# Differential-attention units: output, squares and emission one step later in the attention pipeline

## The chip, the cores and the metric

The kernel runs on one core of a Trainium2 chip. The metric is the device time of one execution in microseconds (us). A core has a matrix engine (TensorE, PE in the profile; PEld is its weight load), a vector engine (VectorE, DVE), a scalar engine (ScalarE, ACT), GpSimd (POOL) and a queue that issues transfers (SyncE, SP). Each engine takes its instructions strictly in order. Matmuls and transposes write to PSUM, of which the kernel uses eight banks of 128 x 512 floats; the other engines read the results from there.

## The reference

Two layers of a decoder trunk on a sequence of 1024 rows of width 1024. Each layer projects the normalised stream to the columns of three groups of heads, runs them, gates them, and maps them back. Only group A is touched by the change:

```python
s1 = jnp.einsum('bhqd,bhkd->bhqk', q1b, k1).astype(jnp.float32) * scale
s2 = jnp.einsum('bhqd,bhkd->bhqk', q2b, k2).astype(jnp.float32) * scale
p1 = jax.nn.softmax(jnp.where(causal, s1, -jnp.inf), axis=-1)
p2 = jax.nn.softmax(jnp.where(causal, s2, -jnp.inf), axis=-1)
w = (p1 - lam * p2).astype(v.dtype)
oa = jnp.einsum('bhqk,bhkd->bhqd', w, v)
...
oa = oaf * lax.rsqrt(jnp.mean(jnp.square(oaf), -1, keepdims=True) + SUBLN_EPS) * subln_g * (1.0 - lam_init)
ya = _from_blocks(oa) * jax.nn.silu(ag)
```

Group B is softmax attention with a forget bias, group C stick-breaking attention. Then `h = LayerNorm(alpha * h + y @ w_out)`.

## The kernel before

**Units and blocks.** In each layer attention is cut into eight units that follow each other: C0, C1 (a pair of heads each), A0, A1, A2, A3 (one differential head each), B0, B1 (a pair each). A unit has eight blocks of 128 query rows. Block i of group A has i+1 key tiles, so blocks grow from 0 to 7; B runs from 7 down to 0.

**Stages of a block (`attn_a`).** `soft` makes two sets of scores on TensorE (tiles S), a maximum and a shift on VectorE (`neg_max`, L300), the exponential on ScalarE (L331), and combines both softmaxes into one weight tile e_A (L334 to L336, VectorE). `turn` transposes that tile on TensorE (tiles T, L310) and copies it back over e_A: the first 512 columns on ScalarE (L312), the rest on VectorE (L314). `mix` multiplies it with the values on TensorE (tile O_A) and copies the result to ou_A (L352, VectorE). `close`, once for four blocks, has ScalarE square the four results (sq_A, L363), GpSimd raise to the power -1/2 (rsa_A, L367) and VectorE scale them (L369). `emit` transposes the four (To_A, L378) and writes y_A (L379, VectorE).

**The steps.** `advance` makes one step: it starts one new block and runs the later stages of blocks that were started before. How many steps behind its start a block's stage runs is the table LAG (soft, turn, mix, close, emit); the order of the stages in one step is ORDER, which is emit, close, mix, soft, turn:

```python
LAG = {"A": (0, 2, 3, 4, 6), "B": (0, 1, 2, 3, 5), "C": (0, 1, 2, 3, 5)}
DEEPEST, LAST = 6, 4
ORDER = {"A": (4, 3, 2, 0, 1), "B": (4, 3, 2, 0, 1), "C": (4, 3, 2, 0, 1)}
```

**Steps between projections.** Beside a unit the kernel computes the projections that later units need (FOLLOW): beside A1 these are q and k of A2 and the gate of A0, beside B0 q of B1, the gate of A3 and k of B1. A step is put between matmuls of the projection (tiles acc_...; acr_... for values) whenever the attention's share of its estimated time falls behind the projection's share. A gate needs its unit finished: before it, steps are made until the unit's last block has been emitted, with no projection between them. The q and k of group A go through the rotary tables on VectorE (L275 to L278) and are then split into two parts, one on ScalarE (L204), one on VectorE (L206 for k, L208 for q).

**Buffers and order.** A scheduler lays the written program out on each engine and hands out buffers; it may take a later matmul before an earlier one that it holds not to be ready. What matters here: "T" has two PSUM banks, and T, O_A, To_A and O_B all live in them; "S" has four banks; "e" has six buffers in SBUF (a block of A takes two in `soft` and keeps one until `mix`; a block of B takes two and keeps both until `mix`).

Of the kernel before, what the change touches and what calls it, by code (L numbers as in the profile page):

```python
# [39 lines left out]
SCORE_US = [2 * sum(0.0945 if b - a == P else (b - a) / 2370 for a, b in row_pieces((i + 1) * P)) for i in range(NB)]  # L40

PACE = 8.0
LAG = {"A": (0, 2, 3, 4, 6), "B": (0, 1, 2, 3, 5), "C": (0, 1, 2, 3, 5)}
DEEPEST, LAST = 6, 4
ORDER = {"A": (4, 3, 2, 0, 1), "B": (4, 3, 2, 0, 1), "C": (4, 3, 2, 0, 1)}
PARTNER = list(range(8, 16)) + list(range(8)) + list(range(16, 32))

# [2 lines left out]
def tile_trunk(ctx, tc, x, ln_in_g, ln_in_b, w_in, b_forget, lambda_q1, lambda_k1, lambda_q2,  # L50
# [581 lines left out]
    for layer in range(DEPTH):  # L632
# [66 lines left out]
        def advance():  # L699
            nonlocal cursor  # L700
            cost = 0.0
            for stage in ORDER[pipe[min(cursor, len(pipe) - 1)][0][0]]:
                for at in range(max(0, cursor - DEEPEST), min(cursor + 1, len(pipe))):
                    u, blk = pipe[at]
                    if cursor - at != LAG[u[0]][stage]:
                        continue
# [97 lines left out]
```

## Time and profile before

| what | us |
|---|---|
| median of 3 executions | 1359.32 (1358.81 to 1362.91) |
| the profiled execution | 1358.92 |
| its span, first to last instruction | 1357.1 |
| TensorE busy in the span | 1323.9 |
| VectorE busy | 858.4 |
| ScalarE busy | 581.1 |
| GpSimd busy | 304.8 |

The profiled execution lies 0.40 below the median, and 1.8 of it lie outside the span. Busy times of engines overlap. The end of a matmul in the profile is modelled, so start times of following matmuls tell more than durations. Times in the rows below are counted from the start of the span.

### The profile page before, as it was taken

The page shows a single profiled execution, that of the slowest core. Times are in us where ns is not written, and L with a number is a line of the kernel's source. Part 1 is how long each engine was busy: PE and PEld are TensorE (multiplying, and loading weights), DVE is VectorE, ACT ScalarE, POOL GpSimd, SP SyncE. Part 2 cuts the span into 40 slices and gives each one's busy share as a digit, 9 for nine tenths or more (in the row PEclk, how much of TensorE's full clock was granted, in tenths as well). Part 3 has the DMA queues.
Part 4 walks back from the last instruction along what each step waited for, and adds up shares of the span by engine and source line. Part 5 has one row for each costly group of instructions (what it writes and reads, how often), then busy time and mean ns, then how long its engine had stood idle before and what let it go on. Part 6 is the DMA issues. An engine that isn't in the chain of part 4 may idle for free.

```text
span 1357.1 us, 21998 instructions
## 1 busy us (share of the span) xinstructions
PE 1323.9 (98%) x8258; PEld 1132.8 (83%) x8258; DVE 858.4 (63%) x1913; ACT 581.1 (43%) x1329; POOL 304.8 (22%) x313
## 2 busy tenths in 40 slices
PE   8999999999999999999999999999999999999997
PEld 6988888987898888877798898898789888888886
DVE  6635577569765775856532538574887657768554
ACT  3345454435444544541214444544444545556100
POOL 4220211111122131233412111012111212221432
PEclk9999999999999999999999999999999999999999
DMA  7551212121213232243515111112121222232332
GB/s 268 167 162 42 63 40 67 48 66 40 63 28 103 55 94 64 101 125 129 171 70 156 47 48 40 55 48 78 40 56 47 65 81 63 63 117 101 119 134 82
DMA packets 116342, 115.41 MB, mean 85 GB/s; under 512 B 8646, under 2 KB 94602, under 8 KB 116236
## 3 DMA queue, kind: packets, MB, share of 16 engines
q1 hardware_dynamic: 116236, 114.01, 28.3%
q8 instruction: 65, 1.06, 0.3%
q14 instruction: 41, 0.34, 0.1%
HBM read 74.63 MB, written 22.05 MB: 71 GB/s over the span
## 4 chain that ended last, share of the span: by engine, by line
PE 45%; DVE 5%; ACT 2%; DMA 2%; issue 1%; POOL 0%; DVEq 0%; ACTq 0%; POOLq 0%; SPq 0%
PE aco_o L72 11%; PE acr_vvA L72 3%; PE acc_ggA L72 3%; PE acc_qA L72 3%; PE O_A L72 2%; PE S_A L72 2%; PE acc_kA L72 2%; PE acr_vvC L72 2%; PE acc_ggB L72 2%; PE acc_kB L72 2%; PE acr_vvB L72 2%; PE acc_ggC L72 1%; PE acc_qB L72 1%; PE acc_kC L72 1%; PE O_C L72 1%
## 5 line engine op out<-in xcount | busy, mean ns | idle before, releaser
L72 PE MATMUL aco_o<-wo,yhi_o 128*128 128x512 f32 (+1 forms) x462 | 141.9, 389 | 0.0
L407 DVE TENSOR_TENSOR_SCAN f_C<-f_C,mask 128x128 f32<-128x128 f32 (+7 forms) x64 | 87.8, 1411 | 40.4 <-ACT f_C L405 40.1
L331 ACT ACTIVATE e_A<-e_A,nm_A 128x256 f32<-128x256 f32 (+7 forms) x128 | 98.9, 773 | 33.6 <-DVE nm_A L300 33.0
L72 PEld LDWEIGHTS aco_o<-wo,yhi_o 128*128 128x128 f32 x462 | 85.3, 188 | 19.0
L72 PE MATMUL aco_o<-wo,ylo_o 128*128 128x512 f32 (+1 forms) x231 | 89.4, 387 | 0.0
L72 PE MATMUL acr_vvA<-whi_vvA,hT 128*128 128x256 f32 x448 | 83.5, 284 | 0.6 <-DVE K_kC L206 0.6
L72 PE MATMUL S_A<-K_kA,Q_qA 128*128 128x384 f32 (+3 forms) x384 | 83.5, 353 | 0.0
L72 PE MATMUL acc_ggA<-hT,whi_ggA 128*128 128x512 f32 x256 | 82.9, 402 | 0.0
L72 PE MATMUL acc_qA<-hT,whi_qA 128*128 128x512 f32 x256 | 82.7, 402 | 0.0
L72 PE MATMUL acc_kA<-hT,whi_kA 128*128 128x512 f32 x256 | 82.5, 402 | 0.0
L363 ACT ACTIVATE sq_A<-ou_A 128x128 f32<-128x128 f32 x64 | 19.9, 311 | 141.4 <-DVE ou_A L352 141.1
L72 PEld LDWEIGHTS O_A<-v_vA,e_A 128*128 128x128 f32 x576 | 73.4, 194 | 7.8 <-ACT e_A L312 4.7
L72 PE MATMUL O_A<-v_vA,e_A 128*128 128x128 f32 x576 | 76.1, 278 | 3.9 <-ACT e_A L312 3.9
L300 DVE CUSTOM_DVE_ANT_0 e_A<-S_A,mask 128x512 f32<-128x512 f32 (+3 forms) x128 | 68.7, 554 | 4.5 <-PE S_A L72 3.1
L72 PEld LDWEIGHTS acr_vvA<-whi_vvA,hT 128*128 128x128 f32 x448 | 69.8, 189 | 1.0 <-DVE K_kC L206 0.8
L72 PEld LDWEIGHTS S_A<-K_kA,Q_qA 128*128 128x128 f32 x384 | 62.9, 189 | 5.0 <-issue 0.3
L395 POOL TENSOR_TENSOR negc<-negc,mask 128x128 f32<-128x128 f32 x64 | 34.0, 534 | 147.0 <-DVE nm_B L300 102.9
L405 ACT ACTIVATE f_C<-S_C 128x384 f32<-128x384 f32 (+3 forms) x96 | 40.8, 493 | 59.2 <-PE S_C L72 58.9
L548 POOL TENSOR_TENSOR ylo_o<-yr_o,yhi_o 128x256 fp32r<-128x256 f32 (+2 forms) x48 | 39.5, 851 | 105.3 <-ACT yhi_o L547 105.1
L399 ACT ACTIVATE e_B<-e_B,nm_B 128x1024 f32<-128x1024 f32 (+7 forms) x64 | 49.6, 776 | 31.4 <-DVE nm_B L300 27.8
L72 PE MATMUL acr_vvA<-wlo_vvA,hT 128*128 128x256 f32 x224 | 63.1, 282 | 0.0
L565 DVE SCALAR_TENSOR_TENSOR r_o<-r_o,aco_o 128x512 f32<-128x512 f32 (+1 forms) x33 | 22.2, 671 | 59.6 <-PE aco_o L72 59.6
(225 smaller groups left out, 3468.1 us busy)
## 6 DMA issues: line engine op xcount, KB each, us to landing
Q_qA<-Q_qA SPq DMA_DIRECT2D x64, 128.0 KB, 2.6
wor<-in_w_out_dram SPq DMA_DIRECT2D x32, 256.0 KB, 3.0
r_o<-h_dram SPq DMA_DIRECT2D x16, 512.0 KB, 3.2
h_dram<-x SPq DMA_DIRECT2D x8, 512.0 KB, 3.4
wr_vvA<-in_w_in_dram SPq DMA_DIRECT2D x16, 256.0 KB, 2.8
Q_qC<-Q_qC SPq DMA_DIRECT2D x32, 128.0 KB, 2.3
wr_qA<-in_w_in_dram SPq DMA_DIRECT2D x16, 256.0 KB, 3.2
wr_kA<-in_w_in_dram SPq DMA_DIRECT2D x16, 256.0 KB, 2.8
```

What stands on the lines that cost most here:

```text
L72: recent[0] = nc.tensor.matmul(*args, **kw).ins
L300: nc.vector.tensor_tensor_reduce(e[:, a:b], sc, other[:, a:b], -1.0, lowest, ALU.add, ALU.min, nm)
L331: nc.scalar.activation(e[:, :n], e[:, :n], AF.Exp, bias=nm, scale=-1.0, accum_out=z)
L363: nc.scalar.activation(t, ou[:, b, :], AF.Square, scale=P ** -0.5, accum_out=ss[:, b:b + 1])
L395: nc.gpsimd.tensor_tensor(diag, diag, mask[:, D:], ALU.add)
L399: nc.scalar.activation(w[:, :n], w[:, :n], AF.Exp, bias=nm, scale=-1.0, accum_out=z)
L405: nc.scalar.activation(w[:, a:b], p, AF.Sigmoid, scale=-1.0)
L407: nc.vector.tensor_tensor_scan(fr, fr, mask[:, :n], 0.0, ALU.mult, ALU.max)
L548: nc.gpsimd.tensor_tensor(ylo[:, e0:e0 + en, :], raw, f32(yhi[:, e0:e0 + en, :]), ALU.subtract)
L565: nc.vector.scalar_tensor_tensor(r[:, c0:c1], r[:, c0:c1], ALPHA, acc, ALU.mult, ALU.add)
```

## The change

The numbers of group A in the table of lags, and the number of steps that `advance` looks back:

```diff
 PACE = 8.0
-LAG = {"A": (0, 2, 3, 4, 6), "B": (0, 1, 2, 3, 5), "C": (0, 1, 2, 3, 5)}
-DEEPEST, LAST = 6, 4
+LAG = {"A": (0, 2, 4, 5, 7), "B": (0, 1, 2, 3, 5), "C": (0, 1, 2, 3, 5)}
+DEEPEST, LAST = 7, 4
```

A block of A is still turned two steps after its start. Its output is now made two steps after the turn instead of one, and its squares, scaling and emission also come one step later. Nothing is added or removed.

What that makes of the engines' order is shown at three places, all in layer 0; layer 1 has the same. In the names, S_A01_4_0_384 is layer 0, head A1, block 4, first softmax, columns from 384; ggA00 is the gate of A0.

First TensorE in unit A1, from the turn of block 1 to the scores of block 4. Before:

```order
L310 MATMUL T_A01_1_0_3152<-ident_69,e_A01_1_0_2966 128x128 x2
...
L72 MATMUL O_A01_1_3171<-v_vA00_1273,e_A01_1_0_2966 128x128 x2
L72 MATMUL S_A01_4_0_0_3175<-K_kA01_0_2322,Q1_qA01_0_1_2239 128x384
...
L310 MATMUL T_A01_2_0_3204<-ident_69,e_A01_2_0_3041 128x128 x3
```

and now:

```order
L310 MATMUL T_A01_1_0_3134<-ident_69,e_A01_1_0_2951 128x128 x2
...
L72 MATMUL O_A01_0_3183<-v_vA00_1273,e_A01_0_0_2898 128x128
L72 MATMUL S_A01_4_0_0_3187<-K_kA01_0_2322,Q1_qA01_0_1_2239 128x384
...
L310 MATMUL T_A01_2_0_3216<-ident_69,e_A01_2_0_3028 128x128 x3
```

Left out are 15 projection matmuls between the turn and the output before, 18 now, and the other scores. The output that stands there is no longer that of the block turned last, but of the one turned a step earlier.

Second, VectorE in the same unit, around the emission of the second half of A0. Before:

```order
L206 TENSOR_TENSOR K_kA02_0_3215<-praw_kA02_0_3209,K_kA02_0_3215 64x512
L206 TENSOR_TENSOR K_kA02_1_3216<-praw_kA02_0_3209,K_kA02_1_3216 64x512
L379 TENSOR_SCALAR y_A00_2061<-To_A00_7_3240,sg_0_898 128x512
L352 COPY ou_A01_0_3131<-O_A01_2_3246 128x128
L300 ISA e_A01_5_0_3257,nm_A01_5_0_0_3258<-S_A01_5_0_0_3251,mask_70 128x384
```

and now:

```order
L336 SCALAR_TENSOR_TENSOR e_A01_5_0_3246<-e_A01_5_1_3258,c_A01_5_3265,e_A01_5_0_3246 128x768
L206 TENSOR_TENSOR K_kA02_0_3159<-praw_kA02_1_3281,K_kA02_0_3159 64x512
L206 TENSOR_TENSOR K_kA02_1_3160<-praw_kA02_1_3281,K_kA02_1_3160 64x512
L379 TENSOR_SCALAR y_A00_2061<-To_A00_7_3291,sg_0_898 128x512
L352 COPY ou_A01_0_3185<-O_A01_2_3297 128x128
L300 ISA e_A01_6_0_3308,nm_A01_6_0_0_3309<-S_A01_6_0_0_3302,mask_70 128x512
```

L379 stood behind the split of the first half of k and ahead of block 5; now it stands behind all of block 5 and the split of the second half, and the turn that takes its bank next is that of block 4 instead of block 3. On TensorE that turn now has 15 gate matmuls (acc_ggA00) ahead of it, and block 6 follows block 5 with only 6 projection matmuls between.

Third, TensorE where unit B0 begins, from the last output of A3 to the outputs of B0's first blocks. Before:

```order
L72 MATMUL O_A03_7_5135<-v_vA02_2390,e_A03_7_0_4879 128x128 x8
L72 MATMUL S_B00_5_0_0_5145<-K_kB00_0_4678,Q1_qB00_0_1_4544 128x384
...
L72 MATMUL S_B00_4_0_0_5268<-K_kB00_0_4678,Q1_qB00_0_1_4544 128x384
...
L72 MATMUL O_B00_7_5234<-e_B00_7_0_4967,v_vB00_3820 64x128
...
L310 MATMUL T_B00_5_0_0_5300<-ident_69,e_B00_5_0_5152 128x128 x4
L72 MATMUL S_B00_3_0_0_5320<-K_kB00_0_4678,Q1_qB00_0_0_4481 128x512
L310 MATMUL T_B00_5_0_512_5306<-ident_69,e_B00_5_0_5152 128x128 x2
```

and now:

```order
L72 MATMUL S_B00_5_0_0_5132<-K_kB00_0_4622,Q1_qB00_0_1_4534 128x384
...
L72 MATMUL O_A03_7_5210<-v_vA02_2386,e_A03_7_0_4860 128x128 x8
L72 MATMUL O_B00_7_5220<-e_B00_7_0_4959,v_vB00_3802 64x128
...
L72 MATMUL S_B00_4_0_0_5254<-K_kB00_0_4622,Q1_qB00_0_1_4534 128x384
...
L310 MATMUL T_B00_5_0_0_5286<-ident_69,e_B00_5_0_5139 128x128 x4
L310 MATMUL T_B00_5_0_512_5292<-ident_69,e_B00_5_0_5139 128x128 x2
L72 MATMUL S_B00_3_0_0_5320<-K_kB00_0_4622,Q1_qB00_0_0_4466 128x512
```

The last output of A3 moved behind the scores of B0's block 5. The gate of A3 waits for A3's emission, so B0's blocks down to block 1 now run in one go ahead of it (down to block 2 before).

## Rows read from the trace of the kernel before

**Rows 1.** The page: span, and busy time of the engines with their shares.

```profile
span 1357.1 us, 21998 instructions
...
PE 1323.9 (98%) x8258; PEld 1132.8 (83%) x8258; DVE 858.4 (63%) x1913; ACT 581.1 (43%) x1329; POOL 304.8 (22%) x313
```

**Rows 2.** Waits of PE, whole span: us in total, times, longest.

```profile
PE O_A L72 <- ACT e_A L312: 3.9, 2, 1.9
...
PE T_A L310 <- DVE y_A L379: 2.3, 2, 1.2
...
PE T_A L310 <- DVE ou_A L352: 1.6, 4, 0.5
```

**Rows 3.** The same view, 290 to 345 us (unit A1, layer 0).

```profile
PE O_A L72 <- ACT e_A L312: 1.9, 1, 1.9
PE T_A L310 <- DVE y_A L379: 1.2, 1, 1.2
PE T_A L310 <- DVE ou_A L352: 0.8, 2, 0.5
```

**Rows 4.** Busy time by stretch: length, then PE, PEld, DVE, ACT, POOL (instructions).

```profile
280.00:299.70 19.70, 19.70 (x114) 17.10 (x113) 13.26 (x36) 7.57 (x25) 3.57 (x3) 1.00 0.20 55
299.70:324.10 24.40, 21.10 (x114) 17.39 (x112) 23.40 (x57) 13.33 (x30) 2.65 (x2) 1.00 0.21 55
324.10:341.00 16.90, 16.31 (x90) 13.82 (x91) 14.41 (x45) 9.68 (x24) 4.12 (x3) 1.00 0.26 61
```

**Rows 5.** Timeline of PE, A1: start, us, what, [idle before and its releaser].

```profile
296.31 0.40 PE L72 MATMUL acc_qA<-hT,wlo_qA 128*128 128x512 f32 x1
...
305.60 0.71 PE L72 MATMUL O_A<-v_vA,e_A 128*128 128x128 f32 x4 [1.94 <-ACT e_A L312]
306.06 1.42 PE L72 MATMUL S_A<-K_kA,Q_qA 128*128 128x384 f32 x8
...
307.57 0.71 PE L72 MATMUL acc_kA<-hT,whi_kA 128*128 128x512 f32 x2
...
311.85 0.60 PE L378 MATMUL To_A<-ident,ou_A 128*128 128x128 f32 x4
...
315.90 0.66 PE L310 MATMUL T_A<-ident,e_A 128*128 128x128 f32 x4 [1.17 <-DVE y_A L379]
...
322.83 0.60 PE L310 MATMUL T_A<-ident,e_A 128*128 128x128 f32 x4
...
324.39 0.33 PE L310 MATMUL T_A<-ident,e_A 128*128 128x128 f32 x1 [0.49 <-DVE ou_A L352]
```

**Rows 6.** Timeline of ACT ahead of the wait at 305.60.

```profile
303.77 0.72 ACT L331 ACTIVATE e_A<-e_A,nm_A 128x512 f32<-128x512 f32 x1
304.49 0.71 ACT L331 ACTIVATE e_A<-e_A,nm_A 128x512 f32<-128x512 f32 x1
305.19 0.35 ACT L312 COPY e_A<-T_A 128x256 f32<-128x256 f32 x1
```

**Rows 7.** Timeline of DVE, A1.

```profile
296.88 1.94 DVE L369 TENSOR_SCALAR ou_A<-ou_A,rsa_A 128x128 f32<-128x128 f32 x4 [1.12 <-POOL rsa_A L367]
...
299.73 0.74 DVE L275 STREAM_SHUFFLE xy_qA<-acc_qA 128x512 f32<-128x512 f32 x1
...
311.31 0.16 DVE L334 RECIPROCAL c_A<-z_A 128x1 f32<-128x1 f32 x1 [0.38 <-ACT e_A L331]
...
312.68 2.39 DVE L206 TENSOR_TENSOR K_kA<-praw_kA,K_kA 64x512 fp32r<-64x512 f32 x2
315.10 0.75 DVE L379 TENSOR_SCALAR y_A<-To_A,sg 128x512 f32<-128x512 f32 x1
...
322.73 1.41 DVE L206 TENSOR_TENSOR K_kA<-praw_kA,K_kA 64x512 fp32r<-64x512 f32 x2
...
324.06 0.28 DVE L352 COPY ou_A<-O_A 128x128 f32<-128x128 f32 x1
```

**Rows 8.** Waits of PE, 485 to 520 us (end of A3, start of B0).

```profile
PE T_B L310 <- ACT e_B L312: 0.2, 1, 0.2
```

**Rows 9.** Timelines of DVE and ACT, start of B0.

```profile
497.99 0.16 DVE L366 TENSOR_TENSOR rsa_A<-rsa_A,ss_A 128x4 f32<-128x4 f32 x1
...
499.28 0.50 DVE L369 TENSOR_SCALAR ou_A<-ou_A,rsa_A 128x128 f32<-128x128 f32 x1
...
507.88 0.83 ACT L399 ACTIVATE e_B<-e_B,nm_B 128x640 f32<-128x640 f32 x1
...
508.73 0.59 ACT L312 COPY e_B<-T_B 128x512 f32<-128x512 f32 x1
```

## The prediction

> **What bounds the kernel now.** I read the page first: TensorE is busy for 1323.9 of 1357.1 us, and no other engine comes near [rows 1]. So the kernel is one long queue of matmuls, and the change leaves their number as it is. It can gain only where TensorE stands still, some 33 us in all, and lose only by new stands. Next I read who TensorE waits for. Three lines name group A: outputs that wait for ScalarE's copy of the turned weights, and turns that wait for VectorE to empty a bank, either the emission y_A or the output copy ou_A. Together these are 3.9 + 2.3 + 1.6 = 7.8 us [rows 2]. The same view cut to unit A1 of layer 0 holds 1.9 + 1.2 + 0.8 = 3.9 [rows 3], half of it; layer 1 has the other half at the same place. Units A0, A2 and A3 have next to none. So what the change can give is decided in two stretches of some 40 us.
>
> Why A1? The table of stretches shows it: from 299.7 to 324.1 VectorE is busy for 23.40 of 24.40 us, while TensorE has only 21.10 [rows 4]. Here the rotary work of q and k meets the softmax of the large blocks. VectorE is late, and TensorE waits for it in three disguises. The first is the 1.94 us at 305.60, before the output of block 1 [rows 5]: the copy that it needs stands on ScalarE behind two exponentials of block 3, and starts at 305.19 [rows 6]. These exponentials waited for VectorE. The second, 1.17 us at 315.90, is the turn of block 3, which takes the bank of To_A; VectorE empties that bank (L379) only at 315.10, behind a split of k that took 2.39 us [rows 5, 7]. The third, 0.49 at 324.39, is the second half of the next turn, behind the output copy at 324.06 [rows 5, 7]. The remaining 0.3 is of the same kind.
>
> **The change part by part.** *The direct wait goes.* At 305.60 the output now belongs to block 0, turned a step earlier, whose copy is long done. 1.94 us per layer, 3.9 in all. By itself that is certain: nothing else held this output.
>
> *The emission moves behind more work.* L379 now stands behind all of block 5 and the split of the second half of k. In the old trace VectorE is through with that list at 324.06. From 299.73 on it had one idle gap of 0.38 [rows 7], so it cannot be much quicker with the same list. Two things shift it. The square scaling L369 (1.94 us after a wait of 1.12 for GpSimd [rows 7]) now falls into this list: +3.1. In exchange the list can begin earlier. The last matmul of q's second half starts at 296.31 and lasts 0.40 [rows 5]; block 7's output, 16 records of 0.115 ((306.06 - 305.60) / 4, rows 5) or 1.8 us, now follows it instead of preceding it, so it is over at 294.9. VectorE took the work up at 299.73 [rows 7], because it was busy with the scaling. Up to 4.8 us are won here. VectorE reaches the end of L379 at about 324.1 + 3.1 - 4.8 = 322.4 (321 if it meets fewer slow splits than the 2.39, 323.5 if the maxima of block 2 hold up its start).
>
> When does TensorE need it? The turn of block 4 stood at 322.83 [rows 5]. Without the two waits ahead of it (3.11) it would be at 319.7. It now has three more projection matmuls ahead of it, 0.24 each ((311.85 - 307.57) / 18, rows 5), and block 3's output, 8 records or 0.9, no longer: 319.5. So about 2.9 us of the 3.1 come back as a wait at block 4's turn, or, a little earlier, as a wait of block 2's output for the bank of block 3's turn. 0.2 us stays won there, between -0.9 (323.5) and 1.6 (321).
>
> *The output copies.* The second half of that turn and a turn later in the unit waited 0.8 us for ou_A [rows 3]. After 324 VectorE's load falls (14.41 of 16.90 [rows 4]), and the scaling that stood between these copies now comes later. I count 0.8 as won; at worst nothing. A1 then gives 1.0 us per layer, with ends of -0.9 and, if every wait goes, 3.9.
>
> *The start of B0.* Today TensorE hardly waits there: 0.2 us are named from 485 to 520 [rows 8]. The change makes the run of blocks without projections one longer and keeps one more buffer of "e" in A's hands: the last weight tile of A3 is held for a step longer, so the second tile of B0's block 5 finds six buffers taken. Its maximum waits on VectorE until the last output of A3 is done, and everything on VectorE queues behind it. Worst off is the copy of B0's second output, behind the scaling L369 that waits for GpSimd. From L366 to L369 was 1.3 us in the old trace [rows 9]. The turn of block 5 needs that bank. I reckon 0.7 us of wait there, and 0.8 at the turn's next tile, whose bank ScalarE empties only after an exponential of 0.83 [rows 9]. Less some 0.6 of short delays that this stretch has already, that is 0.9 lost per layer. No row shows this wait; its bounds are 0 (the cover is there, as today) and 2.5 (three such waits of 0.83, full).
>
> *The rest.* In A2 and A3 the moves are alike, but the key and value work beside them leaves VectorE free, so the cover is there; if it were gone the price would be one bank wait of 1.2 per unit. A gate starts one step later by the steps that must precede it; only A3's is forced to wait, and that is the run just counted. On SP one load of the output weights moves ahead of two transfers of q, and on GpSimd the power moves with the squares; neither queue is waited for by TensorE here. Nothing.
>
> The sum: 2 x (1.0 - 0.9) = 0.2 us less, from 1358.92 of the profiled execution, which lies 0.40 under the median. **The forecast is 1359.1, no change.** The bounds of the parts add up to -7.8 and +6.8. Independent parts seldom stand at their ends together, so this case by itself reaches from 1355.5 to 1363. A measurement of this kernel can tell about 0.3% from no change: 4.1 us, so faster means below 1355.2 and slower above 1363.4.
>
> **The rivals.** *All waits of A1 go, and B0 is covered.* The work that is put ahead of the emission may be as elastic as it looks: the list can begin 4.8 us earlier, and the scheduler put 15 gate matmuls ahead of the turn that needs it. Then 7.8 us go: 1351.5. For it speaks that the largest wait is not a matter of VectorE's throughput alone but of the queue on ScalarE; against it, that VectorE has 23.40 of 24.40 us there [rows 4].
>
> *B0 pays more than A1 gives.* The held buffer is the mechanism, its place the second tile of B0's block 5, and it decides if the wait for GpSimd's power falls between the two output copies, as VectorE's order now has it. Price 2.5 per layer; with A1 at 0: 1359.3 + 5 = 1364.3. For it: six small blocks in one go have nothing to fill a wait. Against: today's five hide nearly all.
>
> *The wait moves whole to the next bank.* TensorE stops at the next claim of one of the two T banks for as long as it stopped at the output: 1359.3. Of the 7.8 us half are already such waits [rows 2], which speaks for it; the sum above has it nearly so for L379, but not for ou_A. [...]
>
> That the change would not do what it says can be left out: the order shows the outputs moved.
>
> **How the numbers follow.** The forecast has 0.45, the moved wait 0.15; both are no change, with some of the forecast's own spread past either bound. The rival of all waits gone has 0.23, that of B0 0.17. From these: faster 0.26, same 0.57, slower 0.17. The likeliest time is 1359.1. The range has to reach into both outer cases to leave out no more than 2 in 10: 1352.5 to 1364.
>
> **What would show it.** The line of O_A waiting for e_A L312 should be gone from TensorE's waits, or come back only as a wait of block 2 in A1. A wait of a turn for y_A L379 should stand in A1 at block 4, 1 to 3 us long in each layer; if none is there, the first rival holds. Waits on ou_A should shrink. At the start of B0 turns should wait for y_B L431 or for ScalarE's copies, about 1 us per layer more than before; more than 2 us makes the second rival. The projections and the output stage should take what they took. I am wrong if A1's waits fall by more than 2 us per layer with nothing new at B0, or if TensorE waits at a place not named here.

## The result, and the profile after

The change is slower. Six executions of it have a median of 1369.81 us (1366.18 to 1371.16), six of the kernel before 1360.55 (1358.81 to 1363.06). The ratio is 1.0061, with a 95% interval from 1.0044 to 1.0078: 8 to 9 us. The forecast of 1359.1 was wrong, and the time lies outside its range.

The profiled execution took 1370.82 us. Its page, against [rows 1]:

```profile
span 1369.0 us, 22025 instructions
...
PE 1330.2 (97%) x8258; PEld 1137.4 (83%) x8258; DVE 853.1 (62%) x1913; ACT 582.4 (43%) x1329; POOL 303.2 (22%) x313
```

The span grew by 11.9 us, TensorE's busy time by 6.3, although the number of matmuls is the same. (The two medians lie 9.3 apart: the profiled execution of the change is 1.0 above its median, that of before 1.6 below the median of the six.) So TensorE stands still longer, and it also works more slowly somewhere. The waits of TensorE over the whole span (in total, times, longest) say where it stands, against [rows 2]:

```profile
PE T_B L310 <- DVE y_B L431: 6.6, 2, 3.9
...
PE T_B L310 <- DVE z_B L400: 3.3, 4, 1.1
PE cps L72 <- DMA tri<-in_c_tri_dram: 3.2, 2, 1.7
...
PE acc_kC L72 <- DVE Q_qC L208: 2.0, 1, 2.0
...
PE S_A L72 <- DVE nm_A L300: 1.2, 3, 0.4
...
PE O_A L72 <- ACT e_A L312: 0.9, 2, 0.4
...
PE T_A L310 <- DVE y_A L379: 0.6, 2, 0.3
```

A1 has gained: the three lines of [rows 2] held 7.8 us, and now O_A, T_A and the new S_A hold 2.7 (T_A for ou_A is gone). What is lost stands in the first line: two waits of T_B for y_B at the start of B0, one per layer, 6.6 us where before had 0.2.

The table of stretches shows the slower work. Its columns are the stretch, its length, busy time of PE, PEld, DVE, ACT and POOL, then the granted clock of TensorE, the share of the DMA engines and GB/s. First the change, with the stretch behind the second wait in pieces of 4 us and one piece of 1 us from each layer, then the kernel before:

```profile
500.00:520.00 20.00, 17.32 (x167) 14.46 (x166) 13.39 (x48) 8.41 (x21) 5.87 (x11) 0.91 0.37 93
1180.00:1200.00 20.00, 17.13 (x115) 14.61 (x116) 11.70 (x46) 9.61 (x24) 5.78 (x11) 0.83 0.18 39
...
1180.00:1184.00 4.00, 1.13 (x4) 1.03 (x5) 1.67 (x8) 0.75 (x2) 2.13 (x4) 0.77 0.87 189
1184.00:1188.00 4.00, 4.00 (x16) 3.46 (x16) 3.19 (x13) 2.17 (x6) 0.67 (x2) 0.50 0.01 2
1188.00:1192.00 4.00, 4.00 (x31) 3.43 (x31) 2.40 (x10) 2.48 (x6) 0.92 (x2) 0.88 0.00 0
...
511.00:512.00 1.00, 1.00 (x5) 0.84 (x5) 1.00 (x4) 0.93 (x3) 0.40 (x1) 0.50 0.05 18
...
1182.00:1183.00 1.00, 0.13 (x1) 0.13 (x2) 0.67 (x3) 0.00 (x0) 0.30 (x1) 0.56 0.71 157
```

```profile
500.00:520.00 20.00, 19.70 (x185) 16.55 (x185) 14.99 (x50) 11.36 (x25) 5.88 (x10) 1.00 0.31 80
1180.00:1200.00 20.00, 20.00 (x128) 16.59 (x127) 7.37 (x18) 6.10 (x13) 3.50 (x4) 1.00 0.15 53
```

Behind each of the two waits TensorE's granted clock is 0.50 for some microseconds (510 to 513 in layer 0, 1183 to 1188 in layer 1), and its matmuls take longer: in 1184 to 1188 the mean of a T_B is 420 ns and that of an S_B of 512 columns 628, in 1150 to 1176, at 1.00, they are 278 and 413. As an estimate from the granted clock of the stretches, that is 20 x (1 - 0.91) = 1.8 us and 20 x (1 - 0.83) = 3.4 us of full-speed work. In the second case the clock is already low from about 1182.1 (1.00 in the piece of 1 us from 1181, 0.56 in that from 1182, 0.50 in the next), while TensorE stands until 1182.87, so some 0.4 us of the 3.4 cost nothing: 4.8 us in all. With the waits, 6.6 - 0.2, B0's start costs 11.2 us. A1's gain of 5.1 stands against it. The other 5.8 of the 11.9 us are many small terms: 2.2 more for z_B, of which one wait per layer is new, at B0's last block; 2.4 more for acc_kC (a projection where a layer begins), ht_ps_o (transposes of a layer's output) and cps (sums for the forget bias, which need the loaded tile `tri`); 1.6 by a clock of 0.94 and 0.98 at 400 to 440; and less than 1 us each at other places, some of them gains. Of these, acc_kC and the clock at 400 to 440 also differ between two profiles of the kernel before (last experiment).

**The chain behind the wait.** Where does y_B come from so late? The rows of the change at the start of B0 in layer 0, first TensorE, then SP's queue, GpSimd and VectorE:

```profile
498.99 1.95 PE L72 MATMUL O_A<-v_vA,e_A 128*128 128x128 f32 x16
...
505.91 0.60 PE L310 MATMUL T_B<-ident,e_B 128*128 128x128 f32 x4
509.19 0.44 PE L310 MATMUL T_B<-ident,e_B 128*128 128x128 f32 x2 [2.68 <-DVE y_B L431]
```

```profile
501.42 1.01 SPq L512 DMA_DIRECT2D negc<-c_dram  x2
```

```profile
503.00 0.46 POOL L395 TENSOR_TENSOR negc<-negc,mask 128x128 f32<-128x128 f32 x1 [2.04 <-DVE nm_B L300]
507.19 0.45 POOL L395 TENSOR_TENSOR negc<-negc,mask 128x128 f32<-128x128 f32 x1 [3.73 <-DMA negc<-c_dram]
507.60 1.01 POOL L367 TENSOR_TENSOR rsa_A<-rsa_A,mhalf 128x4 f32<-128x4 f32 x1
```

```profile
504.83 0.16 DVE L366 TENSOR_TENSOR rsa_A<-rsa_A,ss_A 128x4 f32<-128x4 f32 x1
508.65 0.28 DVE L369 TENSOR_SCALAR ou_A<-ou_A,rsa_A 128x128 f32<-128x128 f32 x1 [3.66 <-POOL rsa_A L367]
508.85 0.28 DVE L431 COPY y_B<-O_B 128x128 f32<-128x128 f32 x1
```

Read them backwards. T_B waits for a bank that y_B's copy (L431) empties. The copy stands on VectorE behind the scaling L369, which waits 3.66 us for the power L367. L367 has had its input since 504.99, but it stands on GpSimd behind a mask, L395, and that one waits for a transfer. The transfer is the load of the two bias tiles `negc` of unit B1 (L512); its buffer is the one that held the values of A2 and A3 (line 509: `pair = big("v", ...)`), so it can start only when the last output of A3 is done: the sixteen matmuls at 498.99 end at 500.94, SP issues at 501.42, the data is there at 507.2. In the kernel before the same places read (PE, SP, POOL):

```profile
495.17 1.95 PE L72 MATMUL O_A<-v_vA,e_A 128*128 128x128 f32 x16
```

```profile
497.15 0.99 SPq L512 DMA_DIRECT2D negc<-c_dram  x2
```

```profile
498.23 1.01 POOL L367 TENSOR_TENSOR rsa_A<-rsa_A,mhalf 128x4 f32<-128x4 f32 x1 [3.14 <-DVE rsa_A L366]
...
502.22 0.81 POOL L395 TENSOR_TENSOR negc<-negc,mask 128x128 f32<-128x128 f32 x1 [1.37 <-DMA negc<-c_dram]
```

There the power stood ahead of B1's mask. The change made its last output and its power a step later; the scheduler then put the mask of B1 ahead of the power, and the load that this mask waits for had itself become later (issued at 501.42 instead of 497.15). Layer 1 shows the same chain: L366 at 1177.28, the mask at 1180.87 after 4.97 us for negc, L369 at 1182.33, T_B at 1182.87 after 3.93.

### The profile page after: what moved, and what is told of

Read it like the earlier page. It is cut to its first block, busy times and chain, and to the rows that moved or that the text cites. A ratio compares the mean times of both kernels' runs of the same rounds, so it can differ in the third digit from the quotient of the medians.

```text
span 1369.0 us, 22025 instructions
## 1 busy us (share of the span) xinstructions
PE 1330.2 (97%) x8258; PEld 1137.4 (83%) x8258; DVE 853.1 (62%) x1913; ACT 582.4 (43%) x1329; POOL 303.2 (22%) x313
## 4 chain that ended last, share of the span: by engine, by line
PE 46%; DVE 3%; DMA 2%; ACT 1%; issue 1%; POOL 0%; DVEq 0%; SPq 0%; ACTq 0%; POOLq 0%
PE aco_o L72 11%; PE acr_vvA L72 3%; PE acc_qA L72 3%; PE acc_ggA L72 3%; PE acc_kA L72 3%; PE O_A L72 2%; PE S_A L72 2%; PE acr_vvC L72 2%; PE acc_ggB L72 2%; PE acc_qB L72 2%; PE acc_ggC L72 1%; PE acc_kB L72 1%; PE acr_vvB L72 1%; PE acc_kC L72 1%; PE T_B L310 1%; PE O_C L72 1%
## 5 line engine op out<-in xcount | busy, mean ns | idle before, releaser
L395 POOL TENSOR_TENSOR negc<-negc,mask 128x128 f32<-128x128 f32 x64 | 33.5, 526 | 151.7 <-DVE nm_B L300 99.1
```

What stands on the lines that cost most here:

```text
L395: nc.gpsimd.tensor_tensor(diag, diag, mask[:, D:], ALU.add)
```

## Experiments

**Theory.** The loss arises where A3 hands over to B0: the power stands in GpSimd's queue behind a mask whose load starts only when A3's last output has freed the values' buffer; the clock falls behind the wait. **Rivals.** The prediction's own mechanism (an "e" buffer held longer and the later closing keep VectorE back, whatever GpSimd does); losses in several units; a clock that falls by chance.

**Which unit?** Three kernels give lags by unit or by block. A3 with the lags of before:

```diff
-LAG = {"A": (0, 2, 4, 5, 7), "B": (0, 1, 2, 3, 5), "C": (0, 1, 2, 3, 5)}
+LAG = {"A": (0, 2, 4, 5, 7), "A3": (0, 2, 3, 4, 6), "B": (0, 1, 2, 3, 5), "C": (0, 1, 2, 3, 5)}
...
-                    if cursor - at != LAG[u[0]][stage]:
+                    if cursor - at != LAG.get(u, LAG[u[0]])[stage]:
```

> Units A0 to A2 keep the new lags, A3 gets the lags of before (0, 2, 3, 4, 6). Theory (GpSimd's queue): what the change costs arises only where A3 hands over to B0, because A3's last output frees the values' buffer a step later; what it gives arises in A1. So the wait of T_B for y_B (6.6 us in the change) goes to about 0.2, the granted clock is 1.00 in the slices at 500 to 520 and 1180 to 1200 us, the waits of A1 stay as in the change (O_A for e_A about 0.9, T_A for y_A about 0.6), and the time is 1353 to 1358 us, under before's 1360.6. Rival (the order of A0 to A2 costs as well, by other weight loads or a later exponential): the time stays above 1362 us.

Measured: 1359.09 us, ratio to before 0.998 (0.9967 to 0.9994). The line of T_B for y_B is not in TensorE's list any more, both stretches have a clock of 1.00, and A1's waits are those of the change (0.9, 0.6, and 0.8 for S_A). The time came out a little above the expected stretch: A3's shift cost some 10.7 us (1369.81 - 1359.09), but the shift of A0 to A2 gave only 1.6 us by the medians and 2.7 by the ratio.

The reverse, A3 alone with the new lags (the tuple of before for "A", the new one for "A3"):

> Units A0 to A2 have the lags of before, only A3 the new ones. Theory (GpSimd's queue): A1's waits are those of before (O_A for e_A 3.9, T_A for y_A 2.3, T_A for ou_A 1.6), T_B for y_B is 6 to 7 us with the granted clock below 1.00 behind both waits, and the time is 1369 to 1374 us, at or above the change itself. Rival (the loss comes from several units, A3 being one): 1363 to 1367 us.

Measured: 1376.59 us, ratio 1.0108 (1.0089 to 1.0128). T_B for y_B 7.1; A1's waits are near those of before (3.9 for O_A, 2.1 for ou_A, and for y_A only one of 1.2). A3's shift alone makes a loss, and the rival's 1363 to 1367 is out. The loss came out larger than expected, with the clock at 0.91 and 0.83 in the same two stretches and low in three others (0.91 at 300 to 320, 0.84 at 420 to 440, 0.91 at 740 to 760). Here A3's shift costs 15.9 us (1376.59 - 1360.7), and with A0 to A2 shifted as well 10.7: the parts do not add up, and the 5 us between were not taken apart.

Only the last block of A3 with the lags of before:

```diff
+LAG = {"A": (0, 2, 4, 5, 7), "A3_7": (0, 2, 3, 4, 6), "B": (0, 1, 2, 3, 5), "C": (0, 1, 2, 3, 5)}
...
+                    if cursor - at != LAG.get(f"{u}_{blk[0]}", LAG[u[0]])[stage]:
```

> The change, but A3's last block alone (block 7) has the lags of before, so its output comes in the same step as block 6's. Theory (what costs is that A3's last output frees the values' buffer, and with it starts the load of negc, a step later, and that the power comes later in GpSimd's queue): T_B for y_B is under 0.6 us, L367 stands ahead of B1's masks and the time is that of A3 with all its lags of before, 1356 to 1361 us. Rival (A3's other blocks cost as well): 1363 us or more.

Measured: 1358.66 us, ratio 0.9985 (0.9976 to 0.9995), no wait for y_B. One block of A3's eight carries the whole loss of A3's shift, the one whose output frees the values' buffer. The wait for z_B is 3.6 us here, no smaller than in the change, and 1.1 in the kernel with all of A3 in time, at the same time of execution; so the 2.2 us of z_B that the change has more are not what made it slower.

**Is it GpSimd's queue?** The change with one instruction per layer moved on GpSimd. In the trace the order on TensorE, VectorE and ScalarE is that of the change, instruction for instruction:

```diff
+                    with tc.issue_after(power[0]) if pair else ExitStack(): nc.gpsimd.tensor_tensor(diag, diag, mask[:, D:], ALU.add)
...
+            power[0] = nc.gpsimd.tensor_tensor(rs, rs, mhalf, ALU.pow).ins
```

> The change, with one instruction per layer moved on GpSimd: the power of A3's second half (L367) ahead of the first mask of B1 (L395), which waits for the load of negc; the order on every other engine stays. Theory (the power waits in GpSimd's queue behind a mask whose load starts only when A3's last output has freed the values' buffer): the scaling L369 follows L366 by about 1.1 us as in before, not by 3.7 and 4.9, T_B for y_B falls from 6.6 to under 1.5 us, the clock behind it stays at 1.00, and the time falls by 5 to 11 us to 1359 to 1365 us; the masks of B0 that still stand behind the load may give 1 to 4 us of it back in block 3. Rival of the prediction (the e buffer and the closing of A3 a step later hold VectorE, whatever GpSimd's queue does): T_B for y_B stays above 3 us, the time above 1366 us.

Measured: 1362.48 us, ratio 1.0012 (1.0002 to 1.0022). GpSimd, VectorE and the two stretches now read:

```profile
502.21 1.02 POOL L367 TENSOR_TENSOR rsa_A<-rsa_A,mhalf 128x4 f32<-128x4 f32 x1 [1.61 <-DVE rsa_A L366]
504.59 0.96 POOL L395 TENSOR_TENSOR negc<-negc,mask 128x128 f32<-128x128 f32 x2 [1.37 <-DMA negc<-c_dram]
```

```profile
501.97 0.15 DVE L366 TENSOR_TENSOR rsa_A<-rsa_A,ss_A 128x4 f32<-128x4 f32 x1
...
503.26 0.29 DVE L369 TENSOR_SCALAR ou_A<-ou_A,rsa_A 128x128 f32<-128x128 f32 x1 [1.13 <-POOL rsa_A L367]
```

```profile
500.00:520.00 20.00, 19.26 (x159) 15.49 (x160) 13.48 (x55) 11.24 (x29) 6.43 (x12) 1.00 0.32 85
1180.00:1200.00 20.00, 19.57 (x130) 15.75 (x129) 9.52 (x33) 8.79 (x22) 6.40 (x10) 1.00 0.05 16
```

L369 follows L366 by 1.3 us, as in before; T_B for y_B is 0.2; the clock stays up; 7.3 us come back. The load is as late as it was (issued 0.50 us after A3's last output, 0.48 in the change; the whole profile runs 2.9 us ahead here), the "e" buffer is held as long, and A3 closes as late: the order of two instructions on GpSimd was worth two thirds of the loss. For these two thirds the prediction's own mechanism is out.

Some 3.7 us (1.0012 against 0.9985) lie between this and the kernel with A3's last block in time. Do the masks of B0, which also stand behind the load, make the difference? Both first masks of B1 behind all masks of B0 (`power[0]` holds the last mask of B0 here, not the power):

```diff
+                    with tc.issue_after(power[0]) if pair else ExitStack(): power[pair] = nc.gpsimd.tensor_tensor(diag, diag, mask[:, D:], ALU.add).ins
```

> The change, with both first masks of B1 moved behind all masks of B0 on GpSimd; the order on every other engine stays. Theory: as in the swap, and what B0's masks still wait for behind the load goes too: T_B for y_B under 0.6 us, no wait of S_B or T_B for a mask in B0 over 0.5 us, clock 1.00 in B0, time 1355 to 1360 us, at or under before. If the masks of B0 never waited, the same time as the swap. Rival (the clock falls in B0 by chance from run to run and not by the wait): the slices at 500 to 520 and 1180 to 1200 us still show 0.8 to 0.9.

Measured: 1362.5 us, ratio 1.0013 (1.0003 to 1.0022): the same as the swap, so the masks of B0 did not wait at a price, and the expected 1355 to 1360 was missed. Of the rest, 1.5 us per execution can be named in the profile of the swap (T_B for ScalarE's e_B 1.2 against 0.3, S_B 0.4, y_B 0.2). Waits for e_B at this place are of the kind that the prediction named, so its mechanism may have a share in this third; no run tests that. The other 2 us stay open.

The counter-test goes the other way: the kernel before, where the power is made to wait for that load. On GpSimd a copy of four columns of B1's first tile, 0.19 us, is put ahead of the power of A3's second half (the lines shift by 6):

```diff
+        seen = tiny.tile([P, 4], F32, tag="seen", name=f"seen_{key}", bufs=1)
+        return tc.issue_after(nc.gpsimd.tensor_copy(seen, load[0][:, :4]).ins)
...
+            with late(key, i): nc.gpsimd.tensor_tensor(rs, rs, mhalf, ALU.pow)
```

> The kernel before, with its own lags, and one thing added per layer: on GpSimd a copy of four columns of B1's first mask (so it waits for the load of negc) stands ahead of the power of A3's second half. Theory (the power in GpSimd's queue behind that load is what costs): the load lands at about 502 and 1171 us as in before, so L369 follows L366 by 5 to 6 us and not by 1.3, VectorE's work behind it is late, TensorE waits for VectorE 3 to 4 us per layer at the start of B0, the granted clock falls below 1.00 behind at least one of the two waits, and the time is 1366 to 1374 us. Rival (the changed order on TensorE and VectorE costs, not the power's wait): within 2 us of before.

Measured: 1366.84 us, ratio 1.0048 (1.0032 to 1.0063): 6.5 us slower, with no lag changed. VectorE's scaling and TensorE's first wait of it (O_B, whose weights VectorE copies):

```profile
505.44 0.67 DVE L375 TENSOR_SCALAR ou_A<-ou_A,rsa_A 128x128 f32<-128x128 f32 x2 [2.78 <-POOL rsa_A L373]
```

```profile
506.69 1.75 PE L72 MATMUL O_B<-e_B,v_vB 128*64 128x128 f32 x28 [1.18 <-DVE e_B L320]
```

So a late power makes a loss without any change of lags. This test is less clean than the swap: with the power late, the scheduler also took scores, turns and gate matmuls at the start of B0 in another order on TensorE, and part of VectorE's work, so the rival is weakened here and excluded only by the swap. The waits named below are 4.8 us more than in before, so not all of the 6.5 is accounted for. Two things came out smaller than expected: TensorE's waits are 5.0 us in all (O_B 2.7, T_B for y_B 2.3), 2.5 per layer, and the clock stayed at 1.00 in all four stretches around these waits, of which none was over 1.5 us.

**Where does the gain come from?** Three kernels with the new lags for some of the early units, by the same edit as the first.

> Only unit A1 has the new lags, A0, A2 and A3 those of before. Theory: the gain is A1's alone (O_A for e_A 3.9 falls to about 0.9, T_A for y_A from 2.3 to about 0.6, T_A for ou_A goes), so the time is that of A0 to A2 with the new lags, 1355 to 1360 us, under before by 1 to 5 us. Rival (A0 and A2 carry part of it): the same as before within 1 us.

Measured for A1 alone: 1361.18 us, ratio 1.0005 (0.9993 to 1.0016). The theory that the gain is A1's alone fell. O_A's wait is gone, but the bank waits grew, as TensorE's list shows:

```profile
PE T_A L310 <- DVE y_A L379: 6.1, 2, 3.1
PE T_A L310 <- DVE ou_A L352: 4.3, 2, 2.2
```

> Only A0 has the new lags. Theory: the wait for block 1's exponential belongs to A1's own lag, so O_A for e_A stays at 3.9 us; T_A for y_A gets smaller or larger with A0's later output (0 to 3 us per layer); the time is within 2 us of before. Rival (the gain of the shift is A0's): under 1358 us.

Measured for A0 alone: 1356.97 us, ratio 0.9974 (0.9963 to 0.9984), as the rival said. O_A for e_A is not listed at all, although A1's lags are those of before, so my theory on it fell too: either shift, A0's or A1's, removes this wait; T_A waits 0.8 for y_A and 0.8 for ou_A.

> A0 and A1 have the new lags, A2 and A3 those of before. Theory: A1's waits go only if A0's closing and output (L369, L379) move with A1's turns; with A1 alone shifted T_A waited 3.1 us per layer for A0's y_A. So here O_A for e_A is about 0.9, T_A for y_A under 1, T_A for ou_A under 1 in all, and the time is that of A0 to A2 shifted, 1355 to 1359 us. Rival (A2's shift is needed too): T_A for y_A or ou_A stays above 3 us and the time is that of before.

Measured for A0 and A1 with A2 and A3 as in before: **1352.83 us, ratio 0.9947 (0.9932 to 0.9962)**, faster than both kernels. A1's three lines hold 2.5 us (0.9, 0.8 and 0.8 for S_A), and the wait of cps, 2.7 in before, is not listed. The clock is 1.00 in every stretch of 20 us but the last; in before it is 0.91 at 1080 to 1100, behind cps. 5.3 + 2.7 + 1.8, less 3.2 by which four waits at other places are longer than in before's profile (acc_kC, ht_ps_o, T_C for f_C, acr_vvB), is 6.6 of the 7.2 us between the spans. Why cps no longer waits was not taken apart; with A2 shifted as well (first experiment) it waits 3.2. That comparison says more: with A2 shifted the ratio is 0.998, without 0.9947, and the two intervals do not overlap. So A2's shift, too, costs about 0.3%, some 4.5 us. In the profiles it shows as the wait of cps and as clocks of 0.93, 0.91 and 0.91 at 400 to 420, 720 to 740 and 1080 to 1100, where the kernel with A0 and A1 alone has 1.00. What in A2's order brings these is not shown. So the rival of losses in several units holds in part: A3's is the largest, not the only one.

**How much do profiles of one kernel differ?** The kernel before, unchanged:

> The kernel before, unchanged, for a second profile. If the waits at the border of the layers (acc_kC for Q_qC 0.7 us in before, 2.0 in the change) and the dips of the clock behind the wait of cps differ from run to run, this profile shows other sizes than the first: acc_kC between 0.7 and 3, and a dip at 400 to 440 us or none. If they belong to the kernel, it shows 0.7 and no dip there.

Measured: 1361.08 us, one execution. acc_kC waits 1.8 us and not 0.7, and the clock is low at places where the first profile had 1.00 (columns as above):

```profile
300.00:320.00 20.00, 18.07 (x89) 15.35 (x88) 18.89 (x48) 11.03 (x26) 2.33 (x2) 0.91 0.20 52
960.00:980.00 20.00, 18.07 (x90) 15.46 (x89) 17.36 (x45) 8.85 (x24) 3.58 (x3) 0.91 0.21 53
```

These are the stretches of A1, with the waits of 1.94 us that [rows 3, 5] show. At 420 to 440 the clock is 0.85, so that dip differs from run to run, too. The wait of T_A for y_A, 2.3 us in the first profile, is not listed here. It is also missing in the layer whose A1 has a clock of 0.91 in two other kernels with A0 and A1 as in before (A3 alone shifted, and the counter-test), and stands there with 1.2 us in the layer where the clock is 1.00. So the waits of A1 cost clock in some executions and not in others, the wait for y_A goes where the clock is low, and a difference of 1 to 2 us between two single profiles proves nothing.

## Why the prediction was wrong, step by step

- **The direct wait goes: right.** 3.9 us became 0.9, and it stands at the output of block 2, as the last part of the prediction allowed.
- **The emission: the time on VectorE came out right by luck, the wait was mis-sized.** L379 was foretold to end at about 322.4 and ended at 322.09. But the list began at 296.55, 3.2 us earlier than before and not 4.8, and the scaling in it took 1.6 (0.76 of waiting and 0.88) and not 3.1: two errors that cancel. But TensorE came for the bank not at 319.5, but at 321.85 (it starts at 322.15 after 0.30). So 0.3 us per layer came back, not 2.9. Of the 2.35 us between, 0.85 are the new short waits (S_A 0.41, O_A 0.44), and 0.4 is there before group A begins (its first scores start at 201.64, in before at 201.25); the rest, 1.1, lies ahead of the turn and I did not count it. The foretold wait is real where A0's part stays behind: with A1 alone shifted it is 3.1 us per layer.
- **The output copies: right.** The 0.8 us per layer are gone. A1 gives 2.55 per layer and not 1.0, within the ends that I had set.
- **The start of B0: the right place, the wrong cause and price. This is the step that failed.** I wrote that the copy of B0's second output would stand behind L369, which waits for GpSimd, and took 0.9 us per layer with a bound of 2.5. The waits are 2.68 and 3.93. The failed sentence stands in "the rest": "on GpSimd the power moves with the squares; neither queue is waited for by TensorE here. Nothing." The power did not only move, it moved behind a mask of B1, and that mask's load is tied to the buffer which the moved output frees. L366 to L369, 1.3 us in [rows 9], became 3.8 and 5.0. The bound was taken from the exponentials of 0.83 in [rows 9], the nearest rows; the row that would have set it is that of the load in the kernel before: issued at 497.15, waited for until 502.22, 5 us. The held "e" buffer, my reason, is not the cause of the 7.3 us that the swap gives back, since the swap leaves it as it is.
- **The clock was missing.** The sum has no term for it. Some 4.8 us of the loss in the profiled execution are slower matmuls behind the waits, by the estimate from the clocks of 0.91 and 0.83.
- **A2 was put at nothing, too.** "In A2 and A3 the moves are alike, but the key and value work beside them leaves VectorE free, so the cover is there": by the experiments A2's shift costs some 4.5 us, for a reason that stays open.

The second rival had the condition word for word (the wait for GpSimd's power between the two output copies) and the sign, at 1364.3 instead of 1369.8: it lacked 1.4 us of wait (6.4 against 5) and 4.8 of clock, and it had A1 at 0 where A1 gave 5.1. Its mechanism, the held buffer, is not what the swap shows. The third says that the wait moves whole to the next bank. For the change the measurement decides against it, since 5.1 of A1's 7.8 us went with the same two T banks; for A1 shifted alone the trace agrees, with 10.4 us of bank waits (6.1 + 4.3) in place of 7.8. No run has another number of banks.

## What to carry to other kernels

Before a step is moved, list the buffers that it frees, the loads that wait for them, and then, on every engine's queue, what stands behind the first reader of such a load: a small instruction on an idle engine can hold the critical one (here the power, 1.01 us on GpSimd, for which L369 waited 3.66). Move a stage where the wait is and leave the unit at the hand-over as it is: the same shift gave 0.5% in two units and cost 0.6% in four. And units that share banks have to be reckoned together: A1's shift alone gave nothing, A0's alone 0.3%, both 0.5%, and A2's on top of them took 0.3% away.

## What the runs showed of the hardware

TensorE's clock fell at the long waits at B0: with the stand of 3.93 us up to 1182.87 it was granted 0.77, 0.50 and 0.88 in the three stretches of 4 us from 1180 on, in the last two of which it was busy throughout, so that the wait of 3.93 cost, by the estimate above, some 3 us more. Cut into pieces of 1 us, from 500 to 530 and from 1172 to 1202, the clock around both waits is 0.50 or 1.00 except in the four pieces where it changes (0.85 and 0.94 in layer 0, 0.56 and 0.52 in layer 1). Not every wait costs this: behind waits of up to 1.5 us in the counter-test the clock stayed at 1.00, and behind A1's wait of 1.94 it was 1.00 in one profile of the kernel before and 0.91 in the other. An edit that only shortens waits may thus pay more than the waits themselves (here 4.8 us of clock, an estimate, stand beside 6.4 of waits), and no single profile shows how much.
